# Hybrid attention and SSD layer on one Trainium2 core: dt sums collected in one tile, dt weights split once, first weight loads issued behind the first casts, softplus begun one product sooner

## The chip, the cores and the metric

The kernel runs on one NeuronCore of one Trainium2 chip. Time is device time in microseconds of one execution; three executions of the kernel before took 2038.48, 2035.58 and 2030.0 us, so its median is 2035.58 us. The engines are named as in the profile: PE (TensorE), DVE (VectorE), ACT (ScalarE), POOL (GpSimd) and SP (SyncE, which only issues transfers). An engine works its own queue strictly in the order in which the program wrote it, and a DMA is issued by an instruction that stands in the queue of SP, ACT or POOL.

## What is computed

One decoder layer on 2048 tokens of width 1024, all in float32. One wide projection feeds two branches; the parts that matter here are `dt_raw`, the last 16 columns of that projection (one for each SSM head), and what is made of it:

```python
proj = jnp.einsum('bsd,de->bse', x, w_in[layer])
q, k, v, z_att, z_ssm, xbc, dt_raw = jnp.split(proj, list(SPLITS), axis=-1)
...
dt = jax.nn.softplus(dt_raw.astype(jnp.float32) + dt_bias[layer].astype(jnp.float32))
a = -jnp.exp(a_log[layer].astype(jnp.float32))
...
y = ssd_chunked(xs_h, dt, a, ...)        # uses cumulative sums of dt * a
...
out = jnp.einsum('bse,ed->bsd', mix, w_out[layer])
x = layer_norm(alpha * x + out, ln_g[layer], ln_b[layer])
```

## The kernel before

**Stages.** The projection comes first, as a list of 36 jobs (to about 837 us of the profiled execution). The dilated attention follows (to about 1660 us), then the output projection with its norm. The change touches the projection alone.

**How a job multiplies.** Every matrix product is a block scheme with seven products in place of eight: the token matrix is cut into blocks R11, R12, R21, R22, of which sums are made (T1, T2, T3, T4), and each weight block likewise (A11, A12, A21, A22, and sums of them). A float32 number is split into a high part in the rounded type fp32r and the low rest: ACT makes the high part by a cast, DVE (or POOL) subtracts it to get the low one. So each token block has two tiles, such as TB11h and TB11l, and each of a job's seven products takes high times high, low times high and high times low. The products run in the order of `LEFT`, B11, T1, B21, T2, B22, T4, T3; in job 0 B21 stands ahead of T1. Job 0 multiplies the first half of the tokens with the first half of the v columns (`wide_products`, 128x256 matmuls), job 11 does the same for the second half of the tokens, and job 12 takes that half with the second half of the v columns. The jobs between and after are `products` (128x512 matmuls).

**What sets the order.** Engine queues of PE, DVE, ACT and POOL are written by hand: code runs in program order, and `after(n, f)` puts `f` behind the n-th product from now; `flush()` is called once behind each product. The pieces that prepare the next job (casts, subtractions, loads) are spread over a job's products in this way. SP's queue holds most stores and the token loads. Transfers of SP and ACT are counted on eight semaphores in rotation, and a transfer waits at its issue for the one that had its semaphore before.

**The start.** Lines 738 to 762 load job 0's operands: SP gets A11 in two halves, R11 in three pieces, R21, the dt weights, R12 and R22; ACT gets A12, A21 and A22 ahead of its first cast. Each token block has its raw data in a tile that is later used for another sum, so the profile shows R11 as TT1l, R21 as TT4h, R12 as TT3l and R22 as TT3h. ACT and DVE then split A11 and R11 piece by piece (`two`, `tok.step("B11")`), A12, R21 and the dt weights (`dt[0]`), and then DVE makes the sums S1 and A21 of the weights and T1 of the tokens.

**The dt path.** `steps_of` (line 360) is called for each half of the tokens, in job 0 and in job 11. `halves` splits the 1024x16 dt weights into a tile of 32 columns, 16 high and 16 low (`wdr`), each time anew. `sums` runs eight matmuls of 32 or 16 rows over a token block that is there for the seven products anyway: B11 into bank 0, B21 on top of it in the same bank, T1 into bank 1, B22 on top of that one. Behind B11, B21 and B22 the bank's 32 rows are copied out by ACT, each into a tile `ev` of 128 rows (line 382); `ev` is a ring of six that also holds the evicted products until they are stored. `MORE` (line 733) says behind which product which sums run; in job 11 those of B11 stand behind T1. `turn` turns the three copies by twelve transposes of 32x32, ACT copies the result into `dt4`, DVE adds it up, and SP stores it as `d_dt`. It runs behind the last product of job 0, and of job 11.

**Softplus and decays.** `decays` (line 496) is a generator that runs up to its next `yield` at each call. Its first part has the loads of `d_dt` in another layout (`xr`, eight transfers), then come softplus by a series (`u`, `z`, `h`), `adt`, two matmuls of `adt` with constants on PE (lines 538 and 539) and the transposes of `cs`. It is called nine times in job 12.

Of the kernel before, what the change touches and what calls it, by code (L numbers as in the profile page):

```python
# [9 lines left out]
F32 = mybir.dt.float32  # L10
# [9 lines left out]
NJ = 128  # L20
# [8 lines left out]
def hybrid_layer(ctx, tc, xb, xc, w52, wv, wdt, convw, convb, dtb, alog, dskp, gcol, wout,  # L29
# [41 lines left out]
    with ExitStack() as c1:  # L71
# [14 lines left out]
        def after(n, f):  # L86

            later.setdefault(count[0] + n, []).append(f)
# [270 lines left out]

        def steps_of(p, pool):  # L360

            raw = pool.tile([128, 8, 16], F32, name="wd")
            nc.sync.dma_start(raw, wdt)
            wd = pool.tile([128, 8, 32], F32R, name="wdr")
            got, banks = {}, {0: pp.tile([128, 512], F32, name="pp")}

            def halves():
                nc.scalar.copy(wd[:, :, 0:16], raw)
                nc.vector.tensor_tensor(wd[:, :, 16:32], raw, wd[:, :, 0:16].bitcast(F32), op=OP.subtract)

            def sums(nm):
                c, a, x = {"B11": (0, 0, 0), "T1": (1, 0, None), "B21": (0, 1, 1), "B22": (1, 1, 2)}[nm]
                if c not in banks:
                    banks[c] = ss.tile([128, 512], F32, name="ss")
                ps = banks[c]
                for k in range(4):
                    for j, w in ((0, 32), (1, 16)):
                        nc.tensor.matmul(ps[0:w, :], wd[:, k + 4 * a, 0:w], T[nm][j][:, k],
                                         start=(a == k == j == 0), stop=(k == 3 and j == 1), skip_group_check=True)
                if x is not None:  # L380
                    got[x] = ev.tile([128, 512], F32, name="ev")
                    nc.scalar.copy(got[x][0:32], ps[0:32])

            def turn():
                ps = ss.tile([128, 512], F32, name="ss")
                for x, e in got.items():
                    for r in range(4):
                        nc.tensor.transpose(ps[:, 128 * x + 32 * r:128 * x + 32 * r + 32],
                                            e[0:32, r * NJ:r * NJ + NJ], ident[0:32, 0:32])
                y = pool.tile([128, 3, 4, 32], F32, name="dt4")  # L390
                nc.scalar.copy(y, ps[:, 0:384].rearrange("p (x r c) -> p x r c", x=3, r=4))
                add = lambda o, a, b: nc.vector.tensor_tensor(o, a, b, op=OP.add)
# [3 lines left out]
                nc.sync.dma_start(d_dt[:, 8 * p:8 * p + 8].rearrange("p (x r) c -> p x r c", x=2), z[:, 1:3])  # L396
            return halves, sums, turn

# [96 lines left out]

        def decays(dp):
            ones = dp.tile([128, 128], F32, name="ones")
            nc.gpsimd.memset(ones, 1.0)
# [39 lines left out]
            nc.tensor.matmul(pc[:, 0:256], tri, a2, start=True, stop=True)  # L538
            nc.tensor.matmul(pc[:, 256:512], ones, a2, start=True, stop=True)
            nc.vector.tensor_copy(cs, v3(pc[:, 0:256]))  # L540
            nc.vector.tensor_tensor(een, v3(pc[:, 256:496]), cs[:, 0:15], op=OP.subtract)
# [190 lines left out]

        MORE = {0: {n: (n,) for n in ("B11", "T1", "B21", "B22")}, 11: {"T1": ("B11", "T1"), "B21": ("B21",), "B22": ("B22",)}}
        E = mybir.EngineType
        cps, sub = ExitStack(), ExitStack()
        cp = cps.enter_context(tc.tile_pool(name="cpa", bufs=1, side="right", reuse_waits="tile"))
        with tc.manual_schedule(engines={E.PE, E.DVE, E.Activation, E.Pool}):
# [8 lines left out]
            load("A11", nc.sync, (2, 3))  # L746
            tok.load("R11", nc.sync, (2, 3), 2)
            load("A12", nc.scalar)
            tok.load("R21", nc.sync)
            load("A21", nc.scalar)  # L750
            load("A22", nc.scalar)
            dt = steps_of(0, vr)
            tok.load("R12", nc.sync)
            tok.load("R22", nc.sync)
            two(0, "A11", (0, 1))
            tok.step("B11", (0,))
            tok.step("B11", (1,))
            two(0, "A11", (2, 3))
            tok.step("B11", (2, 3))
            two(2, "A12")  # L760
            tok.step("B21")
            dt[0]()
            nc.sync.dma_start(ident, cst[:, 0:128])
# [9 lines left out]
            dts = late.tile([128, 16, 16], F32, name="dts")  # L773
            cs = late.tile([128, 16, 16], F32, name="cs")
            een = late.tile([128, 15, 16], F32, name="een")
# [5 lines left out]
            for t, fs in enumerate(((4, 5, "T2r"), ("T2",), ("B22", 6, "T3r"), ("T4r", "T4", 7), ("T3", 8))):  # L781
                for f in fs:
                    after(t, wsteps[f] if isinstance(f, int) else lambda f=f: tok.step(f))
            after(6, dt[2])
            for j in range(16):
# [4 lines left out]
            for m, (ph, (kind, i)) in enumerate(jobs):  # L790
# [12 lines left out]
                if kind == "v":  # L803
                    if m == 11:
                        dt = steps_of(1, vr)
                        after(0, dt[0])
                        after(6, dt[2])
                        dps = decays(vr)
                    if m == 12:
                        for t in (0, 1, 2, 2, 3, 3, 4, 5, 6):  # L810
                            after(t, lambda: next(dps, None))
                    more = lambda nm, m=m, dt=dt: [dt[1](n) for n in MORE.get(m, {}).get(nm, ())]
                    wide_products(layout[m], fin_v(i, p), m == 0, more)
# [645 lines left out]
```

## Time and profile before

| what | us |
|---|---|
| median of three executions | 2035.58 |
| lowest, highest of them | 2030.0, 2038.48 |
| the profiled execution | 2040.01 |
| its span, first to last instruction | 2037.9 |

The profiled execution is some 4 us above the median. Its own time is 2.1 us more than its span. Shares of the span that an engine was busy: PE 96%, DVE 62%, ACT 55%, POOL 50%. In a row of the timeline the first number is the start in us from the first instruction, the second the time that it took, then come engine (with a q where only its sequencer is at work, as in issuing a DMA), line, operation, output <- inputs and shapes, and in brackets how long the engine sat idle before it and what ended that.

### The profile page before, as it was taken

Reading aid. Unit: us, or ns where it says so; the run is one execution under the profiler, and the core shown is the slowest. Engines: PE = TensorE matmul, PEld = TensorE weight load, DVE = VectorE, ACT = ScalarE, POOL = GpSimd, SP = SyncE. Lnnn points to the kernel's source line nnn. Section 1 sums busy time; section 2 is a strip of 40 time slices with the busy share of each in tenths; the row PEclk is TensorE's granted clock in tenths of the full one; section 3 lists DMA queues with packets and bytes.
Section 4 is the critical chain, followed back from the end, with each engine's and each line's share of the span. In section 5 each row is a group of like instructions: output and inputs, shape, how many; then the busy total and the mean of one; then the engine's idle time right before and its main releaser. Section 6 shows DMA issues by size and latency. Waiting matters only on the chain.

```text
span 2037.9 us, 42696 instructions
## 1 busy us (share of the span) xinstructions
PE 1961.9 (96%) x16024; PEld 1598.2 (78%) x16024; DVE 1271.4 (62%) x3193; ACT 1128.9 (55%) x3066; POOL 1010.1 (50%) x866
## 2 busy tenths in 40 slices
PE   8999999999999999999999999998989989999998
PEld 7888879888888888988888776666766668888886
DVE  7555365777766665644454387787777756665553
ACT  4455333556556774456557488887878742222220
POOL 0366513666646767155555424667766652432222
PEclk9999999999999999999999999999999989999999
DMA  6688665565787776887888756777787799332210
GB/s 265 211 281 298 221 252 215 172 197 173 244 287 276 268 256 241 306 275 249 282 269 272 250 191 198 211 215 227 222 235 223 196 309 298 122 97 103 85 67 31
DMA packets 230286, 447.72 MB, mean 220 GB/s; under 512 B 40192, under 2 KB 112384, under 8 KB 218688
## 3 DMA queue, kind: packets, MB, share of 16 engines
q1 hardware_dynamic: 138352, 190.64, 29.5%
q0 software_dynamic: 43776, 160.49, 23.3%
q10 hardware_dynamic: 47952, 93.87, 15.0%
q8 instruction: 126, 2.06, 0.4%
q14 instruction: 80, 0.66, 0.1%
HBM read 301.91 MB, written 151.39 MB: 222 GB/s over the span
## 4 chain that ended last, share of the span: by engine, by line
PE 83%; DMA 5%; DVE 5%; ACT 4%; issue 2%; SPq 1%; POOL 0%; ACTq 0%; POOLq 0%; DVEq 0%
PE pp L260 13%; PE pp L264 13%; PE pp L262 13%; PE N L1002 6%; PE S L949 4%; PE S L1185 4%; PE S L1187 4%; PE S L1186 4%; PE pp L309 4%; PE T L976 3%; ACT P L961 2%; PE T L1185 2%; PE T L1186 2%; PE T L1187 2%; PE ss L309 2%
## 5 line engine op out<-in xcount | busy, mean ns | idle before, releaser
L217 POOL TENSOR_TENSOR w<-wr,w 128x512 fp32r<-128x512 f32 x217 | 285.4, 1326 | 277.0 <-ACT w L216 182.7
L961 ACT ACTIVATE P<-P,st 128x192 f32<-128x192 f32 (+1 forms) x768 | 323.9, 424 | 71.1 <-DVE st L955 67.2
L252 ACT COPY ev<-pp 128x512 f32<-128x512 f32 x200 | 117.2, 588 | 312.5 <-PE pp L264 275.3
L955 DVE CUSTOM_DVE_ANT_0 P<-S,tb 128x192 f32<-128x192 f32 (+1 forms) x768 | 206.8, 325 | 104.5 <-PE S L949 79.9
L272 DVE TENSOR_TENSOR ev<-pp,ev 128x512 f32<-128x512 f32 x152 | 101.2, 686 | 141.4 <-PE pp L264 91.8
L1093 POOL TENSOR_TENSOR wb<-num,wb 128x2048 f32<-128x2048 f32 x21 | 95.5, 4549 | 116.2 <-ACT P L961 63.1
L216 ACT CAST w<-wr 128x512 fp32r<-128x512 f32 x224 | 134.2, 621 | 28.6 <-DVE wr L211 13.3
L961 ACT ACTIVATION_READ_ACCUMULATOR P<-P,st 128x1 f32 x768 | 145.4, 189 | 0.0
L1002 PE MATMUL N<-PT,v 128*64 128x64 f32 (+1 forms) x1536 | 127.0, 262 | 13.7 <-ACT num L1026 10.4
L978 DVE COPY PT<-T 128x512 f32<-128x512 f32 x192 | 131.8, 687 | 4.0 <-PE T L976 3.9
L976 PE MATMUL T<-ident,P 128*128 128x128 f32 x768 | 129.7, 293 | 0.2 <-DVE PT L978 0.2
L976 PEld LDWEIGHTS T<-ident,P 128*128 128x128 f32 x768 | 83.1, 144 | 48.2 <-issue 23.9
L949 PE MATMUL S<-k,ex 64*64 64x192 f32 (+1 forms) x2048 | 113.8, 331 | 6.8 <-issue 6.8
L1002 PEld LDWEIGHTS N<-PT,v 128*64 128x64 f32 x1536 | 79.4, 139 | 51.8 <-ACT num L1026 20.2
L211 DVE TENSOR_TENSOR wr<-wr 128x512 f32<-128x512 f32 x128 | 113.0, 883 | 9.3 <-DMA wr<-w 5.4
L468 DVE SCALAR_TENSOR_TENSOR ss<-U,cw,ss 128x512 f32<-128x512 f32 x144 | 106.0, 751 | 2.9 <-ACT ss L464 0.6
L1161 DVE TENSOR_REDUCE tb<-P 128x128 f32<-128x1024 f32 x30 | 60.1, 2004 | 45.4 <-ACT P L1158 23.0
L1223 POOL TENSOR_TENSOR k<-k,wb 128x1024 f32<-128x1024 f32 x8 | 25.8, 3229 | 122.7 <-DVE k L1222 122.7
L949 PEld LDWEIGHTS S<-k,ex 64*64 64x64 f32 x2048 | 68.6, 138 | 19.5 <-issue 13.3
L594 ACT ACTIVATE mt<-csb,cs 128x128 f32<-128x128 f32 x256 | 79.0, 395 | 0.9 <-PE ss L634 0.8
L603 DVE TENSOR_TENSOR mt<-mt,ss 128x1024 f32<-128x1024 f32 x32 | 39.0, 1220 | 53.3 <-ACT mt L599 52.8
L260 PE MATMUL pp<-TB11h,w 128*128 128x512 f32 x176 | 69.6, 395 | 0.0
(484 smaller groups left out, 6013.0 us busy)
## 6 DMA issues: line engine op xcount, KB each, us to landing
wr<-w ACTq DMA_DIRECT2D x164, 256.0 KB
d_wc<-w SPq DMA_DIRECT2D x48, 512.0 KB
w<-d_wc POOLq DMA_DIRECT2D x48, 512.0 KB, 5.8
wb<-d_wd SPq DMA_DIRECT2D x48, 512.0 KB
d_wo<-wot POOLq DMA_DIRECT2D x32, 512.0 KB, 4.4
csb<-d_cs ACTq DMA_DIRECT2D x32, 512.0 KB
v<-d_v POOLq DMA_DIRECT2D x16, 1024.0 KB, 7.0
vs<-d_v POOLq DMA_DIRECT2D x16, 960.0 KB, 9.0
```

What stands on the lines that cost most here:

```text
L216: nc.scalar.copy(h, r)
L217: low.tensor_tensor(l, r, h.bitcast(F32), op=OP.subtract)
L260: nc.tensor.matmul(ps, w[:, 0, k], th[:, k], start=start and k == 0, stop=False, skip_group_check=not start)
L262: nc.tensor.matmul(ps, w[:, 0, k], tl[:, k], start=False, stop=False, skip_group_check=not start)
L264: nc.tensor.matmul(ps, w[:, 1, k], th[:, k], start=False, stop=(k == 3), skip_group_check=not start)
L309: nc.tensor.matmul(o, (th, tl)[j == 1][:, k, t], w[:, int(j == 2), k], start=start and r % 2 == k == j == 0, stop=(k == 3 and j == 2), ski ...
L949: nc.tensor.matmul(o, A["q"][d][64 * h:64 * h + 64, blk, 64 * a:64 * a + 64], kv, start=True, stop=True)
L955: nc.vector.tensor_tensor_reduce(P[:, h, cs], sp[h][:, cs], t, -0.125, 3.0e38, OP.add, OP.min, accum_out=stat(A, 0, d, h, blk))
L961: nc.scalar.activation(p, p, AF.Exp, bias=stat(A, 0, d, h, blk), scale=-1.0, accum_out=stat(A, 1, d, h, blk))
L976: nc.tensor.transpose(tp[:, h, i], P[:, h, 256 * i:256 * i + 128], ident)
L978: nc.vector.tensor_copy(pt, tp)
L1002: nc.tensor.matmul(o, l, r, start=start, stop=True, skip_group_check=True)
```

## The change

- The three copies of the dt sums go into one tile `de`, at rows 0, 32 and 64, instead of three tiles of the ring `ev`; `turn` then needs four transposes of 96x128 instead of twelve of 32x32.
- The dt weights are loaded and split once, in job 0, into a tile of the pool `late`; job 11 uses it again. The tile `cs` of the decays takes over its place when it is first written.
- In job 11 the sums over B11 stand directly behind product B11 (`MORE`).
- In job 11 `turn` runs behind product T4 instead of T3, and the first part of `decays` behind T3; in job 12 the other eight parts follow, one product sooner each up to the softplus.
- At the start the loads of A12, A21 and A22 stand on ACT's queue behind the first, second and third cast.

```diff
-        def steps_of(p, pool):
-
-            raw = pool.tile([128, 8, 16], F32, name="wd")
-            nc.sync.dma_start(raw, wdt)
-            wd = pool.tile([128, 8, 32], F32R, name="wdr")
-            got, banks = {}, {0: pp.tile([128, 512], F32, name="pp")}
-
-            def halves():
-                nc.scalar.copy(wd[:, :, 0:16], raw)
-                nc.vector.tensor_tensor(wd[:, :, 16:32], raw, wd[:, :, 0:16].bitcast(F32), op=OP.subtract)
+        def steps_of(p, pool, wd):
+
+            banks = {0: pp.tile([128, 512], F32, name="pp")}
+            e = pool.tile([128, 512], F32, name="de")
...
-                    got[x] = ev.tile([128, 512], F32, name="ev")
-                    nc.scalar.copy(got[x][0:32], ps[0:32])
+                    nc.scalar.copy(e[32 * x:32 * x + 32], ps[0:32])
...
-                for x, e in got.items():
-                    for r in range(4):
-                        nc.tensor.transpose(ps[:, 128 * x + 32 * r:128 * x + 32 * r + 32],
-                                            e[0:32, r * NJ:r * NJ + NJ], ident[0:32, 0:32])
+                for r in range(4):
+                    nc.tensor.transpose(ps[:, 96 * r:96 * r + 96], e[0:96, r * NJ:r * NJ + NJ], ident[0:96, 0:96])
...
+            cs = late.tile([128, 16, 16], F32, name="wdr")
             nc.vector.tensor_copy(cs, v3(pc[:, 0:256]))
...
-        MORE = {0: {n: (n,) for n in ("B11", "T1", "B21", "B22")}, 11: {"T1": ("B11", "T1"), "B21": ("B21",), "B22": ("B22",)}}
+        MORE = {0: {n: (n,) for n in ("B11", "T1", "B21", "B22")}, 11: {n: (n,) for n in ("B11", "T1", "B21", "B22")}}
...
+            two(0, "A11", (0, 1))
             load("A12", nc.scalar)
             tok.load("R21", nc.sync)
+            tok.step("B11", (0,))
             load("A21", nc.scalar)
+            tok.step("B11", (1,))
             load("A22", nc.scalar)
-            dt = steps_of(0, vr)
+            wdraw = vr.tile([128, 8, 16], F32, name="wd")
+            nc.sync.dma_start(wdraw, wdt)
+            wdr = late.tile([128, 8, 32], F32R, name="wdr")
+            dt = steps_of(0, vr, wdr)
...
-            two(0, "A11", (0, 1))
-            tok.step("B11", (0,))
-            tok.step("B11", (1,))
...
                     if m == 11:
-                        dt = steps_of(1, vr)
-                        after(0, dt[0])
-                        after(6, dt[2])
+                        dt = steps_of(1, vr, wdr)
+                        after(5, dt[1])
                         dps = decays(vr)
+                        after(6, lambda: next(dps, None))
                     if m == 12:
-                        for t in (0, 1, 2, 2, 3, 3, 4, 5, 6):
+                        for t in (0, 1, 2, 2, 3, 4, 5, 6):
                             after(t, lambda: next(dps, None))
```

How the queues move at three places. First the head of ACT's queue, before; `w_172` is the tile of A12, `A_176` and `A_178` are A21 and A22, `A_165` is A11:

```order
L185 DMA w_172<-wv 128x1024
L185 DMA A_176<-wv 128x1024
L185 DMA A_178<-wv 128x1024
L216 ACT_TABLE_LOAD
L216 CAST w<-A_165 128x512
L143 CAST TB11h<-TT1l 128x512 x2
L216 CAST w<-A_165 128x512
```

The same place in the changed kernel, where `w_175`, `A_183` and `A_187` are A12, A21 and A22:

```order
L216 ACT_TABLE_LOAD
L216 CAST w<-A_165 128x512
L185 DMA w_175<-wv 128x1024
L143 CAST TB11h<-TT1l 128x512
L185 DMA A_183<-wv 128x1024
L143 CAST TB11h<-TT1l 128x512
L185 DMA A_187<-wv 128x1024
L216 CAST w<-A_165 128x512
```

Each of the three loads now stands behind one cast that waits for data. On SP the load of R21 no longer waits for a semaphore that the load of A12 held.

Second, PE in job 11, from the end of product B11 to the start of product B21, before (a line of dots leaves out further matmuls of the same group):

```order
L309 MATMUL pp<-w,TB11h 128x256
L309 MATMUL pp<-w,TT1h 128x256
...
L378 MATMUL pp<-TB11h,wdr 32x512
L378 MATMUL pp<-TB11l,wdr 16x512
...
L378 MATMUL ss<-TT1h,wdr 32x512
L378 MATMUL ss<-TT1l,wdr 16x512
...
L309 MATMUL ss<-w,TB21h 128x256
```

The same place in the changed kernel, where line 372 is the former 378:

```order
L309 MATMUL pp<-w,TB11h 128x256
L372 MATMUL pp<-TB11h,wdr 32x512
L372 MATMUL pp<-TB11l,wdr 16x512
...
L309 MATMUL pp<-w,TT1h 128x256
...
L372 MATMUL ss<-TT1h,wdr 32x512
L372 MATMUL ss<-TT1l,wdr 16x512
...
L309 MATMUL ss<-w,TB21h 128x256
```

The eight matmuls over B11 moved ahead of product T1; ACT's copy of their bank moved with them, to ahead of the casts of TB21h. DVE's split of the dt weights, which stood behind the low parts of B21 and B22, is gone from job 11.

Third, DVE from the end of job 11 into job 12, before; `dt_2853` is the tile `dt4`, L316 is the addition of an evicted product, L211 a sum of weight blocks:

```order
L316 TENSOR_TENSOR ev<-pp,ev 128x512 x4
L211 TENSOR_TENSOR A_2418<-S_2341,A_2418 128x1024
L392 TENSOR_TENSOR dt_2853<-dt_2853 128x12x16
L392 TENSOR_TENSOR dt_2853<-dt_2853 128x4x16
L211 TENSOR_TENSOR w_2505<-w_2505,A_2418 128x1024
L509 TENSOR_TENSOR xr<-xr,dtbt 128x256
...
L516 TENSOR_TENSOR z<-z,u 128x256
L316 TENSOR_TENSOR ev<-ss,ev 128x512 x2
```

The same place in the changed kernel (lines 383, 501 and 516 are the former 392, 509 and 524):

```order
L383 TENSOR_TENSOR dt_2764<-dt_2764 128x12x16
L383 TENSOR_TENSOR dt_2764<-dt_2764 128x4x16
L316 TENSOR_TENSOR ev<-pp,ev 128x512 x4
L211 TENSOR_TENSOR A_2414<-S_2330,A_2414 128x1024
L211 TENSOR_TENSOR w_2489<-w_2489,A_2414 128x1024
L501 TENSOR_TENSOR xr<-xr,dtbt 128x256
...
L516 TENSOR_SCALAR h<-h 128x256
L316 TENSOR_TENSOR ev<-ss,ev 128x512 x2
```

The additions of `dt4` moved ahead of the last four evictions of job 11, and the part of the softplus that stands ahead of job 12's first additions grew by the first steps of the series. On ACT the two exponential steps of the softplus moved ahead of the evictions of job 12's second product and of one weight cast.

More of the change, by code (lines that the diff above doesn't have):

```diff
@@ L380, in sums @@
                 if x is not None:
-                    got[x] = ev.tile([128, 512], F32, name="ev")
-                    nc.scalar.copy(got[x][0:32], ps[0:32])
+                    nc.scalar.copy(e[32 * x:32 * x + 32], ps[0:32])
             def turn():
                 ps = ss.tile([128, 512], F32, name="ss")
-                for x, e in got.items():
-                    for r in range(4):
-                        nc.tensor.transpose(ps[:, 128 * x + 32 * r:128 * x + 32 * r + 32],
-                                            e[0:32, r * NJ:r * NJ + NJ], ident[0:32, 0:32])
+                for r in range(4):
+                    nc.tensor.transpose(ps[:, 96 * r:96 * r + 96], e[0:96, r * NJ:r * NJ + NJ], ident[0:96, 0:96])
                 y = pool.tile([128, 3, 4, 32], F32, name="dt4")
-                nc.scalar.copy(y, ps[:, 0:384].rearrange("p (x r c) -> p x r c", x=3, r=4))
+                nc.scalar.copy(y, ps[:, 0:384].rearrange("p (r x c) -> p x r c", x=3, r=4))
                 add = lambda o, a, b: nc.vector.tensor_tensor(o, a, b, op=OP.add)
@@ L396, in turn @@
                 nc.sync.dma_start(d_dt[:, 8 * p:8 * p + 8].rearrange("p (x r) c -> p x r c", x=2), z[:, 1:3])
-            return halves, sums, turn
+            return sums, turn
         def split_w(e, hf, raw, t):
@@ L496, in decays @@
         def decays(dp):
+            nonlocal cs
             ones = dp.tile([128, 128], F32, name="ones")
@@ L761, in hybrid_layer @@
             tok.step("B21")
-            dt[0]()
+            nc.scalar.copy(wdr[:, :, 0:16], wdraw)
+            nc.vector.tensor_tensor(wdr[:, :, 16:32], wdraw, wdr[:, :, 0:16].bitcast(F32), op=OP.subtract)
             nc.sync.dma_start(ident, cst[:, 0:128])
@@ L773, in hybrid_layer @@
             dts = late.tile([128, 16, 16], F32, name="dts")
-            cs = late.tile([128, 16, 16], F32, name="cs")
+            cs = None
             een = late.tile([128, 15, 16], F32, name="een")
@@ L783, in hybrid_layer @@
                     after(t, wsteps[f] if isinstance(f, int) else lambda f=f: tok.step(f))
-            after(6, dt[2])
+            after(6, dt[1])
             for j in range(16):
@@ L804, in hybrid_layer @@
                     if m == 11:
-                        dt = steps_of(1, vr)
-                        after(0, dt[0])
-                        after(6, dt[2])
+                        dt = steps_of(1, vr, wdr)
+                        after(5, dt[1])
                         dps = decays(vr)
+                        after(6, lambda: next(dps, None))
                     if m == 12:
-                        for t in (0, 1, 2, 2, 3, 3, 4, 5, 6):
+                        for t in (0, 1, 2, 2, 3, 4, 5, 6):
                             after(t, lambda: next(dps, None))
-                    more = lambda nm, m=m, dt=dt: [dt[1](n) for n in MORE.get(m, {}).get(nm, ())]
+                    more = lambda nm, m=m, dt=dt: [dt[0](n) for n in MORE.get(m, {}).get(nm, ())]
                     wide_products(layout[m], fin_v(i, p), m == 0, more)
```

## The prediction

> **What bounds the kernel now.** The page comes first: the busy shares, and the chain of work that ended last.
>
> ```profile
> span 2037.9 us, 42696 instructions
> PE 1961.9 (96%) x16024; PEld 1598.2 (78%) x16024; DVE 1271.4 (62%) x3193; ACT 1128.9 (55%) x3066; POOL 1010.1 (50%) x866
> PE 83%; DMA 5%; DVE 5%; ACT 4%; issue 2%; SPq 1%; POOL 0%; ACTq 0%; POOLq 0%; DVEq 0%
> ```
>
> PE is busy for 96% of the span and makes up 83% of the chain. What the change saves on ACT, DVE or a queue therefore counts only where PE waits for it. So the waits of PE come second, for the first 360 us, beyond which nothing is edited (us in total, times, longest):
>
> ```profile
> PE pp L309 <- ACT TB11h L143: 8.2, 1, 8.2
> PE pp L378 <- DVE wdr L369: 5.5, 2, 4.7
> PE pp L309 <- ACT w L216: 1.9, 1, 1.9
> PE ss L538 <- issue: 1.9, 1, 1.9
> PE pp L309 <- DVE w L217: 0.8, 1, 0.8
> PE pp L378 <- ACT ev L382: 0.5, 1, 0.5
> ```
>
> These six are all that there is, 18.8 us. The third view sums three stretches (start:end, length, then each engine's busy time, and at the end granted clock, DMA share, GB/s):
>
> ```profile
> 26.34:55.04 28.70, 28.70 (x216) 25.62 (x216) 22.77 (x24) 13.60 (x18) 0.00 (x0) 1.00 0.45 173
> 55.04:65.42 10.38, 7.68 (x49) 7.34 (x50) 5.03 (x8) 2.89 (x5) 0.00 (x0) 0.84 0.37 147
> 262.53:278.41 15.88, 11.21 (x66) 7.87 (x65) 10.65 (x14) 7.34 (x11) 1.06 (x2) 0.89 0.82 310
> ```
>
> The first has no wait and full clock. The other two have waits and a clock of 0.84 and 0.89: here a wait is paid twice, once as idle time and once in slower matmuls behind it.
>
> **Job 11: the weights split once.**
>
> ```profile
> 264.23 1.06 ACT L143 CAST TB21h<-TT4h 128x1024 fp32r<-128x1024 f32 x1 [0.91 <-DMA TT4h<-xb]
> 268.23 2.36 DVE L144 TENSOR_TENSOR TB21l<-TT4h,TB21h 128x1024 fp32r<-128x1024 f32 x2
> 270.50 2.36 DVE L144 TENSOR_TENSOR TB22l<-TT2h,TB22h 128x1024 fp32r<-128x1024 f32 x2
> 273.12 0.64 PE L378 MATMUL pp<-TB11h,wdr 128*32 128x512 f32 x1 [4.67 <-DVE wdr L369]
> 278.41 0.27 PE L309 MATMUL ss<-w,TB21h 128*128 128x256 f32 x1
> 26.34 2.03 PE pp L378 x8
> w<-d_wv POOLq DMA_DIRECT2D x7, 1024.0 KB, 8.9
> ```
>
> Product T1 ends at 273.12 - 4.67 = 268.45; PE then waits for the split of the dt weights, which stands on DVE behind 4.7 us of token splits, and product B21 starts at 278.41, 9.96 us later. Changed, only the 16 dt matmuls stand there. Eight at full clock took 2.03 us in job 0 (the row of the chain), so 16 take 4.1, and **5.9 us go**. What is late next? ACT's copy of the first bank now stands ahead of the casts of TB21h and waits for B11's sums: those end at 262.53 + 2.03 = 264.6, the copy takes 0.6, and the cast starts at 265.2 instead of 264.23. TB21h's first half is there at 266.3, before DVE turns to it at 268.23, so DVE doesn't notice; it is done at 270.59, and B21 now starts near 272.5. The weights of a product come by 1 MB transfers (8.9 us from issue to landing), issued when the product three places before has ended, and a product with its sums lasts over 5.8, so two products cover it. Without that cover I lose at most 1 us. Range 4.9 to 6.2.
>
> **Job 0: the copies in a tile of their own.**
>
> ```profile
> 46.02 1.04 ACT L216 CAST w<-A 128x1024 fp32r<-128x1024 f32 x1
> 48.60 1.41 DVE L316 TENSOR_TENSOR ev<-pp,ev 128x512 f32<-128x512 f32 x2
> 53.32 0.58 ACT L382 COPY ev<-ss 32x512 f32<-32x512 f32 x1 [6.26 <-DMA d_v<-ev]
> 54.45 2.50 DVE L144 TENSOR_TENSOR TT3l<-wr,TT3h 128x512 fp32r<-128x512 f32 x4 [4.44 <-ACT TT3h L143]
> 56.96 1.23 DVE L217 TENSOR_TENSOR w<-A,w 128x1024 fp32r<-128x1024 f32 x1
> 28.36 5.76 PE pp L309 x48
> 58.24 7.17 PE pp L309 x46
> ```
>
> ACT's third copy waits 6.26 us for a buffer of `ev` that a store of d_v still reads. Behind it on ACT stand the four casts of TT3h and a weight cast, behind these on DVE TT3l and the low weights, and product T3 waits for both: 1.9 and 0.8 us. It takes from 55.04 to 65.42, 10.38 us, where T1 took 5.76: 4.6 too much, of which 1.9 is slower clock. Changed, the copy goes on at 47.06; the casts are through near 50, the weight cast near 51; DVE is free at 50.01 and needs 2.50 + 1.23, so all is ready at 53.7, 1.3 us ahead of PE. **4.6 us go**; if something eats these 1.3 us and 1 us more, the clock still falls and 2 remain. Range 2.0 to 4.6.
>
> [...]
>
> **Job 12: softplus a product sooner.**
>
> ```profile
> 318.94 0.38 SPq L396 DMA_DIRECT2D d_dt<-dt  x1
> 328.78 0.43 DVE L509 TENSOR_TENSOR xr<-xr,dtbt 128x256 f32<-128x256 f32 x1 [8.72 <-DMA xr<-d_dt]
> 347.97 0.42 DVE L534 TENSOR_TENSOR adt<-dts,al 128x256 f32<-128x256 f32 x1
> 348.50 0.67 PE L538 MATMUL ss<-adt,tri 128*128 128x256 f32 x2 [1.90 <-issue]
> ```
>
> PE stands 1.90 us for `adt`, which DVE ends at 348.39. The path from the store of `d_dt` to L509 takes 9.8 us, that from there to `adt` 19.6. Store and series start one product, some 5.8 us, sooner against PE, so 3.9 us of slack take the place of 1.9 of wait. **1.9 us go**, range 0 to 1.9. On ACT the exponential steps pass ahead of two evictions and a weight cast; these wait only if `xr` is late (a rival, below). On SP the eight `xr` loads pass ahead of stores, whose buffers are not short once the dt copies have left `ev`.
>
> **The turns.**
>
> ```profile
> 65.42 0.86 PE ss L388 x12
> L976 PE MATMUL T<-ident,P 128*128 128x128 f32 x768 | 129.7, 293 | 0.2 <-DVE PT L978 0.2
> ```
>
> Twelve small transposes take 0.86 us. A 96x128 one is not in the trace; between 0.86 / 12 = 0.07 and the 129.7 / 768 = 0.17 us of a 128x128 one I take the latter, to which it is nearest: 4 x 0.17 = 0.7. Twice, **0.3 us go** (0 to 1.1).
>
> **The start.**
>
> ```profile
> GB/s 0 12 199 354 320 246 315 412 412 416 424 463 434 405 431 410 426 442 332 416 410 418 451 426 418 401 270 33 113 303 289 434 393 47 251 157 111 0 0 0
> 5.14 0.62 ACT L216 CAST w<-A 128x512 fp32r<-128x512 f32 x1 [1.71 <-DMA A<-wv]
> 0.74 4.54 DMA w<-wv
> 5.30 9.00 DMA TT4h<-xb
> 17.68 0.29 DVE wdr L369
> 25.82 0.47 ACT ev L382
> 17.00:26.34 9.34, 7.98 (x59) 6.62 (x57) 9.20 (x10) 4.58 (x6) 0.00 (x0) 1.00 1.03 413
> ```
>
> (One figure for each us from 0; a cast; four pieces of the chain; a stretch as above.) From 7 us on the transfers run at some 420 GB/s, so loads put back can only reorder the bytes. SP's bytes up to R21 are 2.6 MB, ACT's 1.6. With ACT's loads behind casts, SP has the engines alone until about 6 us: at the figures shown the first 0.26 MB are in near 3.2 us, where sharing put them near 4, and the second piece gains more; I estimate the first matmul at 5.7 instead of 8.2. But that is no gain by itself. PE must run B11's dt sums before B21, and these need the split that DVE ends at 17.97, behind both parts of TB21l, so behind R21's landing at 14.30. When? Before, R21 was the last of the 4.2 MB to end: the row's figures add up to 4.2 MB near 13.4 us, and it landed at 14.30. Changed, 1.1 MB of SP's are through at 6 us if the figures stay, and the other 1.5 MB at half of 420 end near 13.1, some 0.2 MB ahead of ACT's last. The dip to 246 in the sixth us, where SP held R21 back until 5.30 (the load of A12, landing at 5.28, had its semaphore), should go as well, which is worth another 0.1 MB. So R21 lands **0.5 us sooner**, range 0 to 1.6 (the upper end is reached if SP's transfers get more than half). DVE is busy for 9.20 of the 9.34 us up to PE's restart at 26.34, so it hands this 0.5 through.
>
> Against it stands the clock. Product B11 ends 2 to 3 us sooner, its sums only 0.5, so PE idles some 2.5 us there in place of 0.8. By the row of 55.04 that is about enough to halve the clock for a while, at 1.9 us, of which the idle 0.5 us that PE spends on the copy at 25.82 takes a part, and it may fall or not. I take **0.2 us** for the start: range -1.2 (nothing gained, 1.9 lost, 0.7 of it hidden) to 1.6. [...]
>
> **The sum.** 5.9 + 4.6 + 1.9 + 0.3 + 0.2 = 12.9 us. The profiled execution, 2040.01, would come to 2027.1. It lies 4.4 above the median of the executions shown; nothing edited explains that, so I take the sum from the median too: 2035.58 - 12.9 = **2022.7 us**.
>
> **The rivals.**
> - [...] Chance 0.12.
> - *The next wait at T3*: ACT, DVE and the weight cast stand within 1.3 us of PE, and one late store or load takes that up. 2.6 less, 2025.3. Chance 0.13.
> - *The softplus doesn't come sooner*: DVE reaches `adt` through evictions that wait for PE, so its start may not matter. 1.9 less, 2024.6. Against it: the last evictions ahead of `adt` end one product, 5.8 us, before PE needs it. Chance 0.10.
> - *Slower*: `xr` is late. In the changed order ACT's exponential steps stand ahead of evictions and a weight cast of job 12, so an `xr` that lands more than about 12 us after my estimate (8 us into job 12) stops ACT, and PE pays 1 us for each us beyond. To end slower than before it must come 12 + 12.9 = 25 us late, where store to landing took 9.8. 2036 and more. For it: SP issues in order, behind stores that wait. Chance 0.04.
> - The forecast itself: 0.61.
>
> **How the numbers follow.** A difference of 0.5%, 10.2 us, is about what a measurement of this kernel can tell from no change: four executions lie between 2030.0 and 2040.0. The forecast and the first rival clear it by some 2.7 us; of their 0.73 I count 0.62 as faster. The second and third clear it barely, of 0.23 I count 0.11. Slower by 0.5% asks for 23 us lost: 0.02, the rest within. The range: all low ends together, 4.9 + 2.0 + 0 + 0 - 1.2 = 5.7, give 2029.9; all high ends, 15.4, from the fastest execution shown, 2030.0, give 2014.6. I take 2015 to 2030.
>
> **What would show it.** No wait of L372 (formerly L378) on DVE in job 11, and B21 some 4 us behind T1's end. T3 of job 0 in 5.8 us, clock 1.00. No wait at the matmul of `adt`. At the start: first matmul before 6.5 us, then an idle stretch ahead of the dt sums, and B21's sums at about 26. Wrong it would be if PE waits for `w` or for ACT's copy `de` in jobs 0, 11 or 12, or if the clock falls in new places.

## The result and the profile after

The changed kernel takes 2017.24 us, the median of 4 runs (2015.94 to 2018.82), against 2032.94 (4 runs, 2030.0 to 2038.48) for the kernel before on the same chip: a ratio of 0.992, 95% interval 0.9894 to 0.9946. That is 15.7 us less, between 11.0 and 21.5 by the interval. The forecast was 12.9 us less, 2022.7 us.

The page of the changed kernel, the three lines that answer to those of before:

```profile
span 2016.8 us, 42661 instructions
PE 1951.7 (97%) x16008; PEld 1591.1 (79%) x16008; DVE 1268.6 (63%) x3192; ACT 1125.0 (56%) x3065; POOL 1010.7 (50%) x866
PE 87%; ACT 5%; DMA 4%; DVE 3%; issue 2%; POOL 1%; SPq 0%; ACTq 0%; POOLq 0%; DVEq 0%
```

PE's part of the chain rose from 83% to 87%: less of the span is spent on what PE waits for. The waits of PE in the first 360 us show which went (us in total, times, longest):

```profile
PE pp L309 <- ACT TB11h L143: 6.4, 1, 6.4
PE pp L372 <- DVE wdr L759: 3.4, 1, 3.4
PE pp L309 <- ACT ev L252: 0.5, 1, 0.5
```

Of 18.8 us, 10.3 are left. The waits of T3, of job 11 and at `adt` are gone. The first wait, for the data of the first matmul, is 1.8 us shorter, and the second, for the dt weights in job 0, has grown from 0.8 to 3.4 us. Two stretches of the changed kernel, product T3 of job 0 and job 11 from the start of T1 to the start of B21 (start:end, length, busy time of PE, PEld, DVE, ACT, POOL, granted clock, DMA share, GB/s):

```profile
56.85:62.60 5.75, 5.75 (x50) 5.75 (x50) 2.73 (x4) 1.21 (x2) 0.00 (x0) 1.00 0.67 265
261.68:269.29 7.61, 7.61 (x57) 6.64 (x56) 7.61 (x9) 5.44 (x7) 0.53 (x1) 1.00 0.99 345
```

PE is busy throughout and has full clock in both. The start is the place that got worse. The chain of the changed kernel (start, length, what):

```profile
3.50 10.58 DMA w<-wv
14.11 1.06 ACT w L216
...
16.33 0.78 DVE TB21l L144
...
17.47 1.22 DVE TB21l L144
18.68 0.21 DVE wdr L759
...
18.94 3.39 PE pp L372 x8
22.33 5.94 PE ss L309 x48
28.27 1.85 PE pp L372 x8
...
62.61 0.33 PE ss L380 x4
```

The load of A12, now issued at 3.50, lands 10.6 us later; before, issued at 0.74, it took 4.5. Its cast stands on ACT ahead of those of TB21h, these ahead of TB21l and of the split of the dt weights on DVE, and PE waits for that split. The two windows around it:

```profile
15.50:18.94 3.44, 0.05 (x1) 0.00 (x0) 3.39 (x4) 1.75 (x3) 0.00 (x0) 1.00 1.02 425
18.94:22.33 3.39, 3.39 (x9) 1.54 (x10) 2.99 (x3) 1.05 (x1) 0.00 (x0) 0.55 1.00 382
```

Behind 3.4 us of idle time the clock is 0.55, and eight matmuls take 3.39 us where eight at full clock take 1.85 (the row of 28.27).

From the first matmul of each stage in the two profiled executions (us from the start; attention is the stage that begins with the score matmuls, output the last one):

| begins | before | after | difference | gained or lost since the row above |
|---|---|---|---|---|
| first matmul | 8.23 | 6.41 | -1.82 | -1.82 |
| sums over B21, job 0 | 26.34 | 28.11 | +1.77 | +3.59 |
| job 1 | 66.20 | 62.72 | -3.48 | -5.25 |
| job 11 | 256.78 | 253.89 | -2.89 | +0.59 |
| job 12 | 311.78 | 302.11 | -9.67 | -6.78 |
| job 13 | 355.33 | 343.43 | -11.90 | -2.23 |
| attention | 1162.22 | 1148.05 | -14.17 | -2.27 |
| output | 1652.45 | 1631.97 | -20.48 | -6.31 |
| end | 2037.89 | 2016.8 | -21.1 | -0.6 |

Up to job 13, where the last edit acts, 11.9 us are gained. Behind it the code is the same in both kernels, and yet 9.2 more go, most of it in attention. Three windows of that stage, each from its first matmul to that of the output stage. The kernel before:

```profile
1162.22:1652.45 490.23, 454.12 (x8226) 334.05 (x8225) 374.50 (x1898) 399.48 (x1761) 308.32 (x236) 0.97 0.75 223
```

The changed one:

```profile
1148.05:1631.97 483.92, 449.32 (x8225) 330.87 (x8225) 374.03 (x1898) 396.90 (x1761) 308.18 (x236) 0.98 0.77 226
```

And the kernel before with the new tile for the dt copies alone (an experiment below):

```profile
1155.95:1636.37 480.42, 446.36 (x8226) 328.97 (x8225) 374.25 (x1898) 396.80 (x1761) 308.15 (x236) 0.98 0.77 228
```

The longest and nearly the shortest attention stage of all twelve profiles belong to two kernels without the full change. The profiled execution of before happened to be a slow one there, so the 6.3 us can't be booked to the change as they stand (more on this below), and the experiments are compared by their marks up to job 13 and by their timed runs.

### The profile page after: what moved, and what is told of

The parts are those of the page before. It is cut to its first block, busy times and chain, and to the rows that moved or that the text cites. A ratio compares the mean times of both kernels' runs of the same rounds, so it can differ in the third digit from the quotient of the medians.

```text
span 2016.8 us, 42661 instructions
## 1 busy us (share of the span) xinstructions
PE 1951.7 (97%) x16008; PEld 1591.1 (79%) x16008; DVE 1268.6 (63%) x3192; ACT 1125.0 (56%) x3065; POOL 1010.7 (50%) x866
## 4 chain that ended last, share of the span: by engine, by line
PE 87%; ACT 5%; DMA 4%; DVE 3%; issue 2%; POOL 1%; SPq 0%; ACTq 0%; POOLq 0%; DVEq 0%
PE pp L260 14%; PE pp L264 13%; PE pp L262 13%; PE N L999 6%; PE pp L309 5%; PE S L946 5%; PE S L1182 4%; PE S L1184 4%; PE S L1183 4%; PE T L973 4%; ACT P L958 3%; PE ss L309 2%; PE T L1182 2%; PE T L1183 2%; PE T L1184 2%
## 5 line engine op out<-in xcount | busy, mean ns | idle before, releaser
L211 DVE TENSOR_TENSOR wr<-wr 128x512 f32<-128x512 f32 x128 | 111.4, 870 | 8.9 <-DMA wr<-w 5.4
L587 ACT ACTIVATE mt<-csb,wdr 128x128 f32<-128x128 f32 x256 | 78.5, 393 | 1.1 <-DMA csb<-d_cs 1.0
L260 PE MATMUL pp<-TT4h,w 128*128 128x512 f32 x176 | 69.6, 395 | 0.0
```

The costliest lines, as they stand in the source:

```text
L260: nc.tensor.matmul(ps, w[:, 0, k], th[:, k], start=start and k == 0, stop=False, skip_group_check=not start)
```

## The experiments

The first question is the start: whether the late loads cost it or the longer wait only mirrors the earlier end of product B11, and what makes A12 late. The second is why the whole gain is above the forecast: three runs take one part of the change each. Timed runs of one group share their runs of the kernel before.

**The changed kernel again, and the old order of the start.** The first is the changed kernel without an edit.

> The changed kernel once more, unchanged, as the yardstick for the three others on this chip and as a second look at the attention stage, which the change does not touch. Theory 1 (its 6.3 us there are chance, by where the 3.41 us clock windows fall): the stage from the first scores to the first output matmul comes out anywhere from 483 to 491 us. Theory 2 (the change makes it shorter in some way): 483 to 485 us again. Total 2015 to 2019 us in both, 13 to 17 below before.

The other puts the loads of A12, A21 and A22 back ahead of the casts:

```diff
-            two(0, "A11", (0, 1))
             load("A12", nc.scalar)
             tok.load("R21", nc.sync)
-            tok.step("B11", (0,))
             load("A21", nc.scalar)
-            tok.step("B11", (1,))
             load("A22", nc.scalar)
+            two(0, "A11", (0, 1))
+            tok.step("B11", (0,))
+            tok.step("B11", (1,))
```

> The changed kernel with the three weight loads of ACT back ahead of its first cast. Theory 1 (the start of the change loses, because A12 lands at 14.1 us and its cast stands ahead of the casts of TB21h): first matmul back at 8.2, the split of the dt weights done near 18.0, no half clock behind it, B21's dt sums at 26.3 instead of 28.1, so 1.8 to 2 us faster than the changed kernel. Theory 2 (the sooner first matmul is worth something): slower than the changed kernel by up to 1.8 us.

The changed kernel again took 2016.6 us (5 runs; ratio 0.9915, 0.9895 to 0.9934), with the old start 2016.94 (6 runs; 0.9922, 0.99 to 0.9944). In the repeat PE waits 3.1 us for the weights, and the sums over B21 start at 27.59. With the old start, two of the waits and the stretch from the first to the second dt sums are:

```profile
PE pp L309 <- ACT TB11h L143: 8.4, 1, 8.4
...
PE pp L372 <- DVE wdr L759: 0.8, 1, 0.8
```

```profile
18.21:26.52 8.31, 7.78 (x56) 6.61 (x56) 8.17 (x8) 4.59 (x6) 0.00 (x0) 1.00 1.03 410
```

The first matmul is 2.0 to 2.2 us later, and the sums over B21 start at 26.52, 1.1 to 1.6 us sooner, at full clock. So the moved loads do cost the start more than the early first matmul brings. Little of it reaches job 13, which begins at 342.26 with the old start, and at 343.43 and 342.19 in the two profiles of the changed kernel: with the old start PE waits 0.9 us at the head of job 11 for an eviction that comes late, and in the two others 0.5 us and not at all. In the timed runs a difference of this size can't be told.

**A12 alone back, and R21 in smaller rows.** The first moves only A12:

```diff
+            load("A12", nc.scalar)
             two(0, "A11", (0, 1))
-            load("A12", nc.scalar)
```

> The changed kernel with only the load of A12 back at the head of ACT's queue; A21 and A22 stay behind casts. Theory 1: A12 lands before 8 us, so nothing stands ahead of TB21h's casts but R21 itself, which SP loads without a wait: the split of the dt weights done at 16.5 to 17.5, B21's dt sums at 24.5 to 26.5, 2 to 3.5 us faster than the changed kernel, and the fastest of these four. Theory 2 (A21 and A22, late in the same way, hold back S1 on DVE): B21's dt sums no sooner than 26.3, so the same as with all three loads up front.

The second leaves A12 late, and loads R21 in two transfers with rows of 4 KB instead of one with 8 KB:

```diff
-            tok.load("R21", nc.sync)
+            tok.load("R21", nc.sync, (0, 1), 2)
+            tok.load("R21", nc.sync, (2, 3), 2)
```

> The changed kernel with R21 loaded as two transfers of 4 KB rows instead of one of 8 KB rows; everything else as in the change. Theory 1 (the engines take rows of the two queues in turn, so 8 KB rows on SP against 4 KB rows on ACT leave ACT's loads about a third or less of the bytes): A12 lands 1 to 2.5 us sooner than 14.1, and the split of the dt weights ends that much sooner than 18.9. Rival (ACT's loads are slow because they start late, whatever the rows): A12 lands within 0.5 us of 14.1.

They took 2017.23 us (6 runs; 0.9913, 0.9893 to 0.9934) and 2015.61 (6 runs; 0.9914, 0.9893 to 0.9936). A12's cast on ACT in the changed kernel (start, length, engine, line, operation, and in brackets the wait ahead of it):

```profile
14.11 1.05 ACT L216 CAST w<-w 128x1024 fp32r<-128x1024 f32 x1 [2.88 <-DMA w<-wv]
15.06 1.99 ACT L143 CAST TB21h<-TT4h 128x1024 fp32r<-128x1024 f32 x2
```

With R21 in rows of 4 KB:

```profile
11.38 1.05 ACT L216 CAST w<-w 128x1024 fp32r<-128x1024 f32 x1 [1.60 <-DMA w<-wv]
```

With A12 alone back at the front:

```profile
10.70 1.05 ACT L216 CAST w<-w 128x1024 fp32r<-128x1024 f32 x1
12.70 2.00 ACT L143 CAST TB21h<-TT4h 128x1024 fp32r<-128x1024 f32 x2 [0.95 <-DMA TT4h<-xb]
```

The same load at the same place on ACT lands 2.7 us sooner when R21, on SP's queue, goes in two transfers with rows of half the size. The DMA records show most of the reason (packets that started in one us, by size):

```
                     SP's queue                 ACT's queue
before   4 to 5 us   66 x 2 KB                  45 x 4 KB
after    9 to 10     32 x 8 KB and 15 x 4 KB    25 x 4 KB
after   10 to 11     35 x 8 KB                  37 x 4 KB
s_r21    9 to 10     46 x 4 KB                  48 x 4 KB
s_r21   10 to 11     52 x 4 KB                  50 x 4 KB
```

In the last three rows the two queues moved about the same number of packets, and a packet was a row of the transfer: with 8 KB rows on one side and 4 KB on the other that is 2 to 1 in bytes (287 KB against 152 KB in the third row; 324 against 102 in the second, where the counts aren't equal). Before, A12's 4 KB rows stood against 2 KB ones and had the larger part (184 KB against 135 KB in the first row). From 11 to 13 us of the changed kernel 125 packets of ACT's queue start beside 123 of SP's, of which 91 are the 512-byte rows of the dt weights.

The share of the engines is not all of it. In the changed kernel A12 is issued at 3.50, and the first packet of ACT's queue starts at 7.59, 4.1 us later, with nothing but SP's packets between; before, it was issued at 0.74 and its first packet started at 2.01, 1.3 us later. With the smaller rows the first packet starts at 7.00, so 0.6 of the 2.7 us lie there. What holds the first packet back for so long wasn't tested.

With A12 back, the sums over B21 start at 25.04, with no half clock at the start (1.00 from 15 to 25 us), and job 13 at 340.39, the earliest of all runs, 1.8 to 3.0 us ahead of the three profiles of the changed kernel. R21 has landed by 12.70 there, 1.6 us sooner than before, and the sums over B21 start 1.3 us sooner than before: with A12 out of the way, a sooner R21 does reach PE, as the prediction had it. With the smaller rows the split is done early too, but product B11 also ends sooner, and the clock falls:

```profile
14.10:16.30 2.20, 0.00 (x1) 0.00 (x1) 2.20 (x4) 0.98 (x2) 0.00 (x0) 1.00 1.03 434
16.30:20.60 4.30, 4.30 (x16) 2.75 (x17) 4.27 (x4) 1.05 (x1) 0.00 (x0) 0.60 1.02 423
```

An idle stretch of 2.20 us was enough here to bring the clock down, to 0.60 in the second row; at T3 of the kernel before it was 2.7 us in two parts, with 0.84.

**The parts one at a time.** Each is the kernel before with one part of the change. The tile for the dt copies:

```diff
+            e = pool.tile([128, 512], F32, name="de")
...
-                    got[x] = ev.tile([128, 512], F32, name="ev")
-                    nc.scalar.copy(got[x][0:32], ps[0:32])
+                    nc.scalar.copy(e[32 * x:32 * x + 32], ps[0:32])
...
-                for x, e in got.items():
-                    for r in range(4):
...
+                for r in range(4):
+                    nc.tensor.transpose(ps[:, 96 * r:96 * r + 96], e[0:96, r * NJ:r * NJ + NJ], ident[0:96, 0:96])
```

> The kernel before with nothing but the tile de (and so four transposes for twelve); start, split of the weights and softplus as before. Theory (the wait for a buffer of ev is what held product T3 of job 0): T3 of job 0 runs in 5.8 us at full clock, first matmul of job 1 at 61.0 to 61.2 instead of 66.2; job 11 still waits 4.7 us for its split; first matmul of job 13 5.5 to 5.8 us sooner than before. Rival (T3 is held by DVE's work behind it, and the ev wait only comes last): job 1 starts no more than 2 us sooner.

The dt weights split once, with the sums over B11 of job 11 left behind T1:

```diff
-        def steps_of(p, pool):
+        def steps_of(p, pool, wd):
...
-            raw = pool.tile([128, 8, 16], F32, name="wd")
-            nc.sync.dma_start(raw, wdt)
-            wd = pool.tile([128, 8, 32], F32R, name="wdr")
...
+            wdr = late.tile([128, 8, 32], F32R, name="wdr")
+            dt = steps_of(0, vr, wdr)
...
-                        dt = steps_of(1, vr)
-                        after(0, dt[0])
-                        after(6, dt[2])
+                        dt = steps_of(1, vr, wdr)
+                        after(6, dt[1])
```

> The kernel before with the dt weights split once and kept for job 11, and nothing else: the sums over B11 still stand behind product T1. Theory (the wait for the split is all): product B21 of job 11 starts 3.7 to 4.1 us behind the end of T1 instead of 9.96, no half clock, first matmul of job 13 5.9 to 6.3 us sooner than before. Rival (moving B11's sums ahead of T1 is needed, since ACT's copy of their bank would come too late): PE waits over 0.5 us at the sums over B21, or B21 starts later than 4.5 us behind T1.

The softplus sooner:

```diff
-                        after(6, dt[2])
+                        after(5, dt[2])
                         dps = decays(vr)
+                        after(6, lambda: next(dps, None))
                     if m == 12:
-                        for t in (0, 1, 2, 2, 3, 3, 4, 5, 6):
+                        for t in (0, 1, 2, 2, 3, 4, 5, 6):
```

> The kernel before with the second turn and the parts of the softplus one product sooner, and nothing else. Theory: no wait at the matmul of adt, first matmul of job 13 1.8 to 2.3 us sooner than before, all else as before. Rival (DVE reaches adt no sooner, since evictions that wait for PE stand in between): the wait of 1.90 us stays above 1. A second rival: with ev as short as before, the sooner turn makes PE wait for its third copy, which would show as a new wait at the transposes.

And the kernel before without an edit.

> The kernel before, unchanged, for a second profile. Theory 1 (the attention stage, first scores to first output matmul, varies by chance between executions): it takes 480 to 490 us, and the 490.2 us of the first profile was at the slow end; in five profiles with the change it took 479.6 to 484.4. Theory 2 (the change shortens it): 489 us or more again. The marks of the projection as in the first profile within 0.6 us; ratio 1.00.

| kernel (10 timed runs each) | median us | ratio to before | by the ratio | priced in the prediction |
|---|---|---|---|---|
| dt tile alone | 2027.16 | 0.9968 (0.9955 to 0.9982) | -6.5 us | 4.6, with the turns 4.9 |
| weights split once alone | 2025.44 | 0.9960 (0.9946 to 0.9973) | -8.1 | 5.9 |
| softplus alone | 2030.01 | 0.9980 (0.9967 to 0.9993) | -4.1 | 1.9 |
| before again | 2032.90 | 0.9991 (0.9977 to 1.0005) | -1.8 | 0 |

The runs of before that these share have a median of 2034.96 us. No interval of the three parts reaches 1, and each gain is some 2 us above its price; but the unedited kernel came out 1.8 below too, so most of this surplus may be that of the group of runs. The softplus alone isn't told from the unedited kernel by time, since their intervals overlap; its gain rests on the trace. The place of each gain is shown by windows. With the dt tile alone: T3 of job 0, the dt wait of job 11, the matmul of `adt`:

```profile
55.30:61.20 5.90, 5.90 (x54) 5.90 (x52) 2.81 (x5) 1.21 (x2) 0.00 (x0) 1.00 0.70 275
258.09:273.95 15.86, 10.95 (x66) 7.81 (x65) 10.86 (x15) 7.27 (x11) 1.06 (x2) 0.89 0.82 303
341.30:346.70 5.40, 3.60 (x15) 3.17 (x14) 3.93 (x9) 1.94 (x5) 1.28 (x1) 0.70 0.30 100
```

With the weights alone, T3 and job 11:

```profile
55.10:65.50 10.40, 7.75 (x50) 7.38 (x49) 5.02 (x8) 2.87 (x5) 0.00 (x0) 0.84 0.38 147
262.65:272.12 9.47, 9.47 (x66) 7.48 (x65) 9.47 (x13) 6.03 (x8) 1.06 (x2) 1.00 1.05 411
```

With the softplus alone, T3 and job 11; at `adt` PE doesn't wait:

```profile
55.30:67.00 11.70, 9.03 (x51) 8.69 (x50) 5.01 (x8) 2.87 (x5) 0.00 (x0) 0.71 0.34 129
264.06:280.31 16.25, 12.27 (x67) 8.21 (x66) 10.98 (x13) 8.11 (x11) 1.06 (x2) 0.79 0.87 323
```

Before again, all three:

```profile
55.10:64.40 9.30, 6.61 (x56) 6.26 (x55) 5.04 (x8) 2.89 (x5) 0.00 (x0) 1.00 0.44 168
261.83:279.09 17.26, 12.10 (x66) 8.14 (x65) 12.00 (x15) 8.11 (x11) 1.06 (x2) 0.80 0.80 298
347.60:353.00 5.40, 3.48 (x14) 3.22 (x15) 3.91 (x9) 1.83 (x5) 1.27 (x1) 0.72 0.28 97
```

Each part removes its own wait and none of the others: T3 runs in 5.9 us, job 11's stretch in 9.47, and PE doesn't wait at `adt`. The marks up to job 13 don't add up as neatly. Job 13 begins 3.7 us sooner than in the first profile with the dt tile alone, 6.3 with the weights alone and 0.2 with the softplus alone, where 5.5 to 5.8, 5.9 to 6.3 and 1.8 to 2.3 were expected, and in the second profile of before it begins 2.6 us later. The waits that stay show most of the reason: the same 2.7 us of idle time at T3 (length less PE's busy time) goes with a clock of 0.84, 0.84, 0.71 and 1.00 in four executions, and the 1.8 to 2.3 us at `adt` with 1.00 in the first profile and with the weights alone, and 0.72 and 0.70 in two others. The stretch around `adt` in the first profile:

```profile
346.60:352.00 5.40, 3.50 (x26) 3.43 (x27) 3.80 (x9) 2.38 (x5) 1.51 (x2) 1.00 0.28 97
```

What differs is where the idle time lies. The trace holds the clock that was granted at each time. Within an execution all stretches of half clock begin whole steps of 3.413 us apart (in the first profile at 58.07 and 273.11, 63 steps), and from one execution to the next these steps lie elsewhere. Cut along the steps, T3 in the first profile of before:

```profile
54.65:58.07 3.42, 0.89 (x6) 0.48 (x4) 3.41 (x5) 3.28 (x6) 0.00 (x0) 1.00 0.45 156
58.07:61.48 3.41, 3.24 (x15) 3.24 (x16) 2.01 (x4) 0.00 (x0) 0.00 (x0) 0.50 0.73 305
```

And in the second one:

```profile
53.01:56.42 3.41, 2.10 (x18) 1.90 (x16) 1.90 (x4) 3.03 (x6) 0.00 (x0) 1.00 0.47 154
56.42:59.83 3.41, 2.03 (x14) 1.82 (x15) 3.37 (x5) 1.57 (x3) 0.00 (x0) 1.00 0.52 186
59.83:63.24 3.41, 3.41 (x31) 3.41 (x30) 0.35 (x1) 0.00 (x0) 0.00 (x0) 1.00 0.50 202
```

In the first, 2.53 us of the idle time fall into one step, and the next step has half clock. In the second the idle time falls into two steps, 1.31 and 1.38 us, and no clock is lost. In the first 360 us of the twelve profiles, once the clock is up, 14 steps at full clock have 1.79 us or more of idle time, and half clock follows each; of the 1194 with 1.63 or less it follows none. Over the whole traces the border is less sharp: half clock follows all 69 steps with over 2 us, none of the 6722 with under 1.2, and 32 of the 93 between.

From job 12 to job 13, which holds the wait at `adt`, the four profiles that still have this wait take 43.55, 45.44, 44.99 and 43.50 us, those without it 41.32 both in the softplus run and in the changed kernel.

**Both edits of the start together.** A12 ahead of the casts, and R21 in two transfers; the changed kernel once more beside it.

```diff
+            load("A12", nc.scalar)
             two(0, "A11", (0, 1))
-            load("A12", nc.scalar)
-            tok.load("R21", nc.sync)
+            tok.load("R21", nc.sync, (0, 1), 2)
+            tok.load("R21", nc.sync, (2, 3), 2)
```

> The changed kernel with both remedies at the start: the load of A12 at the head of ACT's queue, and R21 as two transfers of 4 KB rows. Theory (A12 early and rows of one size both take the wait for A12 away, and with less bytes taken by R21's rows A21 and A22 land sooner): split of the dt weights done by 16.2, no half clock behind it, B21's dt sums at 24.5 to 25.0, first matmul of job 13 at 339.5 to 341 against 342.2 and 343.4 in the two profiles of the changed kernel, so 2 to 3 us sooner. Rival (the two remedies are one and the same, and the chain is then bound by DVE alone): as with A12 early alone, 340.4. Total: 2 to 3 us below the changed kernel's, which five rounds can hardly tell apart.

> The changed kernel once more beside it, unchanged, as its yardstick on this chip: 2015 to 2019 us, and a half clock of 3.41 us ahead of B21's dt sums again if an idle time of 3.1 to 3.4 us sets it off by rule and not by chance.

The first took 2018.51 us (6 runs; 0.9917, 0.9898 to 0.9937), the second 2016.99 (6 runs; 0.9912, 0.9896 to 0.9928). The two edits don't add up. Two pieces of the chain with A12 alone at the front, a load of the weight blocks that S1's sum needs and that sum on DVE:

```profile
7.91 8.57 DMA A<-wv
...
16.58 1.24 DVE S L211
```

With both edits:

```profile
8.18 10.63 DMA A<-wv
...
18.91 1.24 DVE S L211
```

and the stretch that follows there:

```profile
24.29:27.36 3.07, 0.00 (x0) 0.00 (x0) 2.97 (x4) 2.93 (x5) 0.00 (x0) 1.00 0.87 368
27.30:30.80 3.50, 3.44 (x9) 1.45 (x10) 3.47 (x4) 1.05 (x2) 0.00 (x0) 0.51 0.38 128
```

A21 and A22 land 2.1 us later, DVE forms the sum 2.3 us later, and PE waits 3.1 us ahead of the sums over B21, with half clock behind. Job 13 starts at 344.78, later than in all three profiles of the changed kernel (343.43, 342.19, 343.16).

## Why the prediction was right, and where it was not

- **Job 11** (5.9 us, 4.9 to 6.2): right in the mechanism, half a us small and just above its range. The stretch from the end of product B11 to the start of B21 went from 15.88 to 9.47 us, 6.4 less: eight dt matmuls at full clock take 1.85, not the 2.03 of the row that I took. B21 starts 1.85 us behind T1's end, not some 4: I counted all 16 matmuls there, though eight of them now stand ahead of T1. The run with the weights alone leaves them behind T1 and has the same 9.47, so their place brings nothing in this stretch.
- **Job 0, T3** (4.6): 10.38 became 5.76, 4.6 us. The cover of 1.3 us held, in all runs with the new tile. That the price holds on average too is seen from B21's sums to job 1: the four profiles with the old copies take 39.86, 38.44, 39.96 and 41.15 us, a mean of 39.85, beside 39.86 in the profile that I read.
- **The turns** (0.3, 0 to 1.1): a size off, 1.1. Four 96x128 transposes take 0.33 us, 0.08 each, the lower of my two bounds; I had taken the upper.
- **Softplus** (1.9, 0 to 1.9): right; job 12 to 13 shrank by 2.2 us, and no late `xr` appeared.
- **The start** (0.2 gained; 1.2 lost to 1.6 gained): this step failed. 1.8 us were lost in the first profile of the changed kernel, 1.3 and 1.4 in the two others (27.59 and 27.75 against 26.34). In the first, the first dt sums start 0.9 us later than before (18.94 against 18.02), and the rest of the loss is their slower clock. What failed is "these need the split that DVE ends at 17.97, behind both parts of TB21l, so behind R21's landing at 14.30": I let R21's landing alone set the split, while A12's cast, whose load I knew to be moved, stands on ACT between. And "the other 1.5 MB at half of 420" failed: not the bytes but the packets came out about even between the queues (35 beside 37 from 10 to 11 us), and the rows on SP's were twice as long (8 KB beside 4), so A12 was the slow one, after 4.1 us in which no packet of its queue started. The first matmul came at 6.41, 6.21 and 5.93 instead of 5.7: alone, SP's queue moved not the 320 to 354 GB/s of the row of before but 120 from 3 to 5 us. The halved clock, which I gave a price below one full event, fell in all three profiles (0.55 behind the wait in the first; in the first repeat the dt matmuls go from 0.40 to 0.63 us each). It is a clock that falls in a new place, which the prediction named as a sign of being wrong, and for the start it was one.
- **A wait** of 0.5 us at the head of job 11, on an eviction that stands on ACT behind casts whose load was late, wasn't foreseen. It is there in two of three profiles of the changed kernel. The second profile of before waits 0.4 us at the same place, for weights that land late, so a late load there isn't the change's alone.
- **The sum.** By the marks up to job 13 the terms give 6.4 + 4.6 + 1.1 + 2.2 - 1.8 - 0.6 = 11.9 us, the difference in the table, beside 12.9. The means of the repeats give 13.7 there: 356.6 for two profiles of before (355.33, 357.89), 342.9 for three of the changed kernel. In the first profile the parts that came out larger (1.6 us together) made up for most of the 2.6 us by which the start and the new wait fell short. That the sum came so near although one of its terms failed is in part luck.
- **Why the measured gain is above it.** The timed runs show 16 to 18 us in three groups (ratios 0.992, 0.9915 and 0.9912; the intervals together reach from 0.9894 to 0.9946). Up to job 13 the waits that went had cost more on average than in one profile: job 12 to 13 loses 3.1 us against the mean of the four profiles with the wait, 44.37, not the 2.2 against the first; and job 11, 55.00 us in the profile that I read, takes a mean of 55.34 with the old split, in 55.00, 56.48, 54.38 and 55.48. Behind job 13, attention takes 479.6 to 484.4 us in the seven kernels with the whole change, a mean of 482.5, and 480.4 to 490.2 in the five others, a mean of 485.3. These overlap, one profile each is too few, and nothing in the code there differs; whether the 2.8 us between the means are chance or come from the change stays open.
- **The rivals.** The softplus came sooner, no next wait appeared at T3, `xr` wasn't late. The idle time at the start didn't leave the clock alone: it was 3.1 to 3.4 us in the changed kernel, with 0.55 behind it, and 2.20 in the run with the smaller rows, with 0.60.

The order with A12 alone at the front is the better one by the marks (job 13 at 340.39). By its time, 2017.23 us, it can't be told from the changed kernel.

## What to carry to other kernels

A load that is moved to a later place can take a different share of the transfers (A12, issued at 3.50 instead of 0.74, took 10.6 us instead of 4.5), and the work behind its cast moves with it (the split of the dt weights ended at 18.89 instead of 17.97): follow every instruction of the queue behind it up to the one for which the bottleneck waits, not only the transfer that was last before. Price a wait of PE from several executions, since the slower matmuls behind it depended here on where the idle time fell among the steps of the clock (2.7 us at T3 came with 0.71 to 1.00); taking the idle time out took this away as well (T3 in 5.75 us, at 1.00). A first matmul that starts sooner (here by 1.8 us) is worth nothing where later ones wait for the same data (the sums over B21 came 1.8 us later), and it can cost the clock (0.55 behind the wait of 3.4 us).

## What the runs showed of the hardware

- In three stretches in which two queues had work side by side they moved about as many packets each, and a packet was a row: 35 packets of 8 KB beside 37 of 4 KB in one us, 52 beside 50 when both had 4 KB, and 123 beside 125 in two us when most of the first were of 512 bytes. In two others the counts weren't even: 66 beside 45, and 47 beside 25. Halving the rows of a transfer on one queue (and splitting it in two) moved the landing of a load on another by 2.7 us.
- A load that was issued on ACT's queue at 3.50 had its first packet at 7.59, and one that was issued at 0.74 had it at 2.01. In the two repeats the first took 4.0 and 4.1 us; the cause is open.
- SP's queue by itself, mostly with rows of 2 KB, was uneven: 120 GB/s from 3 to 5 us, and 279 and 328 in the two halves of the us before. One figure for each half us of the changed kernel, from 0:

```profile
GB/s 0 0 0 37 279 328 180 82 78 139 229 279 328 336 397 344 414 410 426 426 434 442 379 378 428 457 394 421 430 464 393 418 426 451 401 451 401 412 383 429
```

  Two queues later kept the engines busy throughout, with a DMA share of 1.02 at 425 GB/s (15.50 to 18.94).
- The same idle time doesn't give the same clock: 2.7 us in two parts cost nothing once, one step of half clock twice and two once (1.00, 0.84, 0.84 and 0.71); 3.1 us and more ahead of dt sums cost at least one in every profile (0.55 behind 3.44 us, 0.51 behind 3.07, and 0.79 to 0.89 over the stretch of job 11 where the wait stands). A step lasted 3.41 us (215.04 us for 63 of them), and what counted up to 360 us was the idle time within one step: by the busy time that the profile gives, at 1.79 us and more the next had half clock, at 1.63 and less it hadn't.
